# Raw input into the first two P1 products, its row factor put in at their eviction, and three steps of the last pair's products moved behind the scores

## The chip, the cores and the metric

The kernel runs on one core of one Trainium2 chip. The metric is the device time of one execution in microseconds (us); for the kernel before, it is the median of three runs. TensorE is PE in the rows of the profile, VectorE DVE, ScalarE ACT, GpSimd POOL, and SyncE SP.

## What is computed

Two encoder layers over 512 tokens of width 2048, in float32. Each layer normalises its rows, multiplies by one wide input weight, runs three groups of heads (latent attention, a gated short convolution, attention into 256 memory tokens), gates them and multiplies by an output weight. What the change touches is the first line of a layer and its first products:

```python
def rmsnorm(x, g):
    x32 = x.astype(jnp.float32)
    y = x32 * lax.rsqrt(jnp.mean(x32 * x32, axis=-1, keepdims=True) + EPS)
    return (y * g.astype(jnp.float32)).astype(x.dtype)

    for l in range(DEPTH):
        h = rmsnorm(x, pre_norm_g[l])
        z = h @ w_in[l]
        q_lat, kv_lat, k_pe, gb, gc, xin, q_mem, gate = split_cols(z)
        ...
        a_out = mla_attention(q, k, v)
        ...
        y = jnp.concatenate([a_out, c_out, m_out], axis=-1) * jax.nn.silu(gate)
        o = y @ w_o[l]
        x = x + rmsnorm(o, post_norm_g[l])
```

The row factor of the norm, one number per token, multiplies a whole row. So it can be put in ahead of a product with the weight or behind it.

## The kernel before

**Precision.** Every float32 operand is split into a high part (a rounded copy, made by ACT) and a low part (the rest, made by DVE). A product is three matmuls, high by high, high by low, low by high (`mm3`, lines 250 to 254, so every product shows up as L252, L253 and L254). For a weight block these are `wh` (L177) and `wl` (L178), for the left operand the two lines of `split_to` (L257 and L258).

**Blocks.** The input and the output products are done with seven products of blocks in place of eight (Strassen's scheme). The left operand is cut into halves of the tokens and halves of the contraction: A11, A12, A21, A22, with the sums S1 to S4 made from them by `combine`. P1 multiplies A11, P2 multiplies A12, P5 multiplies S1, and so on (`LEFT`). Each half of the tokens is two tiles of 128 tokens. A `group` covers two column blocks of the weight. For the first two groups of a layer (form `HEAD`) P1 and P2 of both groups come first, and P5 and the rest of both groups after that, because S1 to S4 need the second half of the tokens. A product has four steps of one weight block each (256 rows of the contraction), each step does both token tiles, and each token tile takes six matmuls, so a step is twelve matmuls. The first two steps of the very first P1 are one (`two`): tile 0 by two weight blocks, then tile 1. When a product ends, `ended` evicts its PSUM bank: P1 of these groups is copied by ACT (L464), P2 is added to it by DVE (L457).

**The order.** All steps are recorded by `add` and run by `Program.run` in that order. A step's weight block is loaded some units ahead and prepared (split) two units ahead. TensorE, SP and POOL take their instructions in the recorded order; for ACT and DVE this holds until `first.close`, and after it a scheduler picks their order. Small work such as `combine` and the splits is put into a queue (`pr.defer`) with a cost, and is taken from it as steps with `room` go by, or at once where a product asks for an operand (`pr.until` in `products`). SP carries the loads, POOL carries loads that add to a tile in place (`more`), and the short row factor computation.

**The start.** Per tile of 128 tokens: `first_load` brings x, `first_factor` sums its squares on ACT (L563) and makes the factor on POOL, `first_rows` multiplies on DVE (L613), `transpose_rows` turns it on TensorE (L582) and evicts it with the gain of the norm, by DVE (L584) or ACT (L588), and `left_half` splits it. TensorE turns an identity 60 times meanwhile (`warm`, L1208).

**The end of attention.** `pipeline` runs one iteration per head and query block: the score of iteration k, whatever stands between, the transposes of iteration k-3 (L1002), and for every other one the product with V of iteration k-5. For the last pair of heads, what stands between is P2 of both groups of the output projection, one step per iteration:

```python
        last_pair = {0: [(sums(0), []), g0[0][0]], 1: [g0[0][1]], 2: [g0[0][2]], 3: [g0[0][3]],
                     4: [g1[0][0]], 5: [g1[0][1]], 6: [g1[0][2]], 7: [g1[0][3]]}
```

The pair has eight iterations, 0 to 7. From 8 on no score is left.

## Time and profile before

| | us |
|---|---|
| median of three runs | 1514.81 (1514.28 to 1516.2) |
| the profiled execution | 1515.76 |
| its span, first to last instruction | 1514.0 |
| TensorE busy in it | 1488.7 (98%) |
| DVE busy | 1065.3 (70%) |
| ACT busy | 863.7 (57%) |
| POOL busy | 287.5 (19%) |

The span is counted from the first instruction of the program to the last; the time of an execution has some more around it. Rows of the timeline give the start and the length in us, the engine, the source line, the operation, what is written from what, the shapes and how often; a bracket gives the idle time ahead of it and what ended that. A matmul's length is its way through the array; consecutive ones overlap, so that the distance of their starts is their cost.

### The profile page before, as it was taken

What the parts mean: (1) busy time and instruction counts of PE and PEld (TensorE: products, weight loads), DVE (VectorE), ACT (ScalarE), POOL (GpSimd) and SP (SyncE); (2) the same over time, 40 slices, a digit from 0 to 9 for tenths busy, and PEclk for the clock granted to TensorE, in tenths of its full rate; (3) what the DMA queues carried; (4) which work ended last, traced back from release to release, by engine and by line L of the source; (5) the groups of instructions that cost most, each with busy time, mean ns of one, the idle gap of its engine ahead of it and who ended that gap; (6) DMA issues with size and microseconds to landing.
All of it is one profiled execution on the core that took longest, in us unless ns stands there. A gap on an engine that the chain in (4) does not pass through costs nothing.

```text
span 1514.0 us, 20209 instructions
## 1 busy us (share of the span) xinstructions
PE 1488.7 (98%) x7613; PEld 1277.7 (84%) x7613; DVE 1065.3 (70%) x1422; ACT 863.7 (57%) x1335; POOL 287.5 (19%) x289
## 2 busy tenths in 40 slices
PE   9999999999999999999999999999999999999997
PEld 7788888988898888878788888888988888888885
DVE  6965675565877668769788765675565586688687
ACT  7743534454667768644588533534454587686443
POOL 1233131332000000230220233131333000003111
PEclk9999999999999999999999999999999999999999
DMA  8999898989582111595987999898989521137945
GB/s 329 218 220 224 194 176 169 201 198 250 164 267 76 48 42 57 106 213 155 319 290 236 237 220 222 197 173 171 205 194 213 152 70 43 29 90 138 260 111 181
DMA packets 142581, 267.19 MB, mean 176 GB/s; under 512 B 17084, under 2 KB 39956, under 8 KB 139156
## 3 DMA queue, kind: packets, MB, share of 16 engines
q0 software_dynamic: 59072, 128.99, 44.5%
q1 hardware_dynamic: 83280, 136.88, 28.1%
q8 instruction: 59, 0.97, 0.3%
q14 instruction: 38, 0.31, 0.1%
q10 hardware_dynamic: 132, 0.05, 0.0%
HBM read 251.20 MB, written 14.68 MB: 176 GB/s over the span
## 4 chain that ended last, share of the span: by engine, by line
PE 83%; DVE 6%; issue 4%; ACT 3%; POOL 2%; DMA 1%; POOLq 0%; DVEq 0%; ACTq 0%
PE P L253 20%; PE P L254 20%; PE P L252 20%; PE ptp L1002 2%; PE tps L758 2%; DVE wl L178 1%; PE o L253 1%; PE sc L252 1%; PE sc L253 1%; PE sc L254 1%; PE o L254 1%; PE o L252 1%; POOL wr L137 1%; PE sc L982 1%; PE sc L983 1%
## 5 line engine op out<-in xcount | busy, mean ns | idle before, releaser
L178 DVE TENSOR_TENSOR wl<-wr,wh 128x1024 fp32r<-128x1024 f32 (+1 forms) x400 | 476.0, 1194 | 303.5 <-ACT wh L177 302.7
L177 ACT CAST wh<-wr 128x1024 fp32r<-128x1024 f32 (+1 forms) x400 | 411.9, 1032 | 475.5 <-PE P L254 397.0
L253 PE MATMUL P<-wl,S 128*128 128x512 f32 (+1 forms) x896 | 344.2, 384 | 2.9 <-DVE wl L178 2.8
L252 PE MATMUL P<-wh,S 128*128 128x512 f32 (+1 forms) x896 | 346.1, 386 | 0.0
L254 PE MATMUL P<-wh,S 128*128 128x512 f32 (+1 forms) x896 | 343.5, 383 | 0.0
L137 POOL DMA_DIRECT2D wr<-in_w_in_dram x160 | 193.5, 1209 | 484.4 <-DVE wl L178 380.3
L252 PE MATMUL P<-wh,A 128*128 128x512 f32 (+1 forms) x656 | 253.1, 386 | 0.6 <-ACT wh L177 0.6
L253 PE MATMUL P<-wl,A 128*128 128x512 f32 (+1 forms) x656 | 251.9, 384 | 1.5 <-DVE wl L178 1.5
L254 PE MATMUL P<-wh,A 128*128 128x512 f32 (+1 forms) x656 | 251.6, 384 | 0.5 <-DVE A L258 0.5
L253 PEld LDWEIGHTS P<-wl,S 128*128 128x128 f32 x896 | 168.3, 188 | 33.6 <-DVE wl L178 4.5
L254 PEld LDWEIGHTS P<-wh,S 128*128 128x128 f32 x896 | 168.2, 188 | 30.6
L252 PEld LDWEIGHTS P<-wh,S 128*128 128x128 f32 x896 | 168.1, 188 | 29.6 <-ACT wh L177 0.3
L137 POOL DMA_DIRECT2D wr<-in_w_o_dram x40 | 48.4, 1209 | 527.4 <-DVE rec L990 352.1
L253 PEld LDWEIGHTS P<-wl,A 128*128 128x128 f32 x656 | 123.2, 188 | 23.6 <-DVE wl L178 2.1
L254 PEld LDWEIGHTS P<-wh,A 128*128 128x128 f32 x656 | 123.1, 188 | 23.4 <-DVE A L258 1.2
L252 PEld LDWEIGHTS P<-wh,A 128*128 128x128 f32 x656 | 123.1, 188 | 23.1 <-ACT wh L177 1.5
L988 ACT ACTIVATE P<-sc,nm 128x512 f32<-128x512 f32 (+1 forms) x96 | 60.0, 625 | 36.4 <-DVE nm L985 35.8
L991 ACT ACTIVATE P<-P,rec 128x512 f32<-128x512 f32 (+1 forms) x96 | 62.1, 658 | 5.1 <-DVE rec L990 5.1
L985 DVE TENSOR_REDUCE nm<-sc 128x1 f32<-128x512 f32 (+1 forms) x96 | 57.1, 595 | 10.0 <-PE sc L983 6.2
L258 DVE TENSOR_TENSOR PT<-ptp,PT 128x512 fp32r<-128x512 f32 (+1 forms) x96 | 56.4, 593 | 8.5 <-ACT PT L257 8.1
L182 ACT ACTIVATE wh<-wr,cols 128x512 fp32r<-128x512 f32 x64 | 44.2, 721 | 19.9 <-PE mk L253 7.4
L183 DVE SCALAR_TENSOR_TENSOR wl<-wr,cols,wh 128x512 fp32r<-128x512 f32 x64 | 46.3, 746 | 12.4 <-ACT wh L182 12.2
(272 smaller groups left out, 2225.2 us busy)
## 6 DMA issues: line engine op xcount, KB each, us to landing
wr<-in_w_in_dram POOLq DMA_DIRECT2D x128, 512.0 KB, 6.9
wr<-in_w_in_dram SPq DMA_DIRECT2D x112, 512.0 KB, 5.4
wr<-in_w_o_dram SPq DMA_DIRECT2D x48, 512.0 KB, 4.2
wr<-in_w_o_dram POOLq DMA_DIRECT2D x40, 512.0 KB, 7.3
wr<-in_w_in_dram POOLq DMA_DIRECT2D x32, 416.0 KB, 5.4
wr<-in_w_in_dram SPq DMA_DIRECT2D x24, 416.0 KB, 4.2
wr<-in_w_mk_dram SPq DMA_DIRECT2D x16, 512.0 KB, 4.9
wr<-in_w_mv_dram SPq DMA_DIRECT2D x16, 512.0 KB, 4.9
```

The source lines that it names most:

```text
L137: engine.dma_start(dst, src, **kw)
L177: nc.scalar.copy(hi[:, :n], src)
L178: nc.vector.tensor_tensor(lo[:, :n], src, hi[:, :n].bitcast(F32), op=ALU.subtract)
L182: nc.scalar.activation(hi[:, h], src[:, h], AF.Copy, scale=g)
L183: nc.vector.scalar_tensor_tensor(lo[:, h], src[:, h], g, hi[:, h].bitcast(F32), op0=ALU.mult, op1=ALU.subtract)
L252: nc.tensor.matmul(ps, ah, bh, start=first, stop=False, **kw)
L253: nc.tensor.matmul(ps, ah, bl, start=False, stop=False, **kw)
L254: nc.tensor.matmul(ps, al, bh, start=False, stop=last, **kw)
L258: nc.vector.tensor_tensor(lo, src, hi.bitcast(F32), op=ALU.subtract)
L985: nc.vector.tensor_reduce(nmax, ps, axis=AX.X, op=ALU.max, negate=True)
L988: nc.scalar.activation(pt, ps, AF.Exp, bias=nmax, accum_out=tot)
L991: nc.scalar.activation(pt, pt, AF.Copy, scale=rec)
```

## The change

- The first two tiles are loaded by halves of the columns, with weight blocks between them. Their first halves are turned as they come, without a factor, in quarters that are split one by one (`turn_raw`, `split_raw`). So A11 is raw for P1 of the first two groups of layer 0, and the eviction of these P1 multiplies by the row factor on ACT (`factor`).
- The square sums, factors and scaled second halves of these tiles come later. 28 warm-up transposes take the place of 60, and the second step of the first P2 is joined too (`k < 2`).
- `combine` needs the scaled first halves. Their turned form is multiplied in place by the factors, which are spread over a PSUM bank by two transposes (`spread_factors`, `scale_half`); A11 is split a second time, scaled, after the second group's P1.
- The constants are split into two loads; those of the memory norm and the convolution are issued by SP behind the fourth tile, and turned after the first P2.
- In both layers the last three steps of P2 of the output's second group go from iterations 5, 6, 7 to 8, 9, 10.

```diff
-            if by_two and k == 0:
+            if by_two and k < 2:
                 steps[:2] = [(two(names[0], 0), [unit(names[0], c) for c in range(2)], 0.0, 1)]
...
-                if apart:
+                if apart and factor:
+                    nc.scalar.activation(s[1, 0], ps, AF.Copy, scale=factor(tt))
+                elif apart:
                     nc.scalar.copy(s[1, 0], ps)
...
+    def spread_factors():
+        ps = G["rows01"] = bank("rps")
+        for t in range(2):
+            wide = scrap("factors", P)
+            nc.vector.tensor_copy(wide, G[f"r{t}"].broadcast_to([P, P]))
+            nc.tensor.transpose(ps[:, t * P:(t + 1) * P], wide, G["ident"])
+
+    def scale_half(t, h):
+        r = G["rows01"][:, t * P:(t + 1) * P].rearrange("p (o c) -> p o c", o=1).broadcast_to([P, 8, P])
+        nc.vector.tensor_tensor(h, h, r, op=ALU.mult)
...
     add(setup)
+    add(lambda: first_load(0, (0,)))
+    add(pr.begin_loads(1))
+    add(lambda: first_load(1, (0,)))
+    add(pr.begin_loads(2))
     for t in range(2):
-        add(lambda t=t: first_load(t))
-        add(lambda t=t: first_factor(t))
-        if t == 0:
-            add(lambda: first_rows(0))
-    add(pr.begin_loads(3))
+        add(lambda t=t: first_load(t, (1,)))
+        add(pr.begin_loads(3 + t))
+    add(pr.begin_loads(6))
     add(lambda: first_load(2))
-    add(pr.begin_loads(5))
+    add(pr.begin_loads(8))
     add(lambda: first_load(3))
-    add(lambda: warm(60))
-    add(turn_constants)
+    add(constants_load)
+    add(lambda: warm(20))
+    add(pre_gains)
...
-            add(turn_half(0, 0))
-            add(lambda: first_rows(1, (0,)))
+            def turn_raw(t, q, on=None):
+                return lambda: transpose_rows(0, t, G[f"x{t}"], (q,), on)
+            def split_raw(t, q):
+                return lambda: G["left"].split("A11", t, G[f"hT{t}"][:, 4 * q:4 * q + 4, :], slice(4 * q, 4 * q + 4))
+            add(turn_raw(0, 0))
+            add(turn_raw(0, 1))
+            add(split_raw(0, 0))
             add(pr.begin_prep(1))
-            add(lambda: left_half(0, (0,)))
+            add(split_raw(0, 1))
+            add(lambda: warm(8))
+            add(turn_raw(1, 0))
             add(pr.begin_prep(2))
-            add(turn_half(1, 0, nc.scalar))
-            add(lambda: first_rows(1, (1,)))
-            add(lambda: left_half(1, (0,)))
+            add(turn_raw(1, 1, nc.scalar))
+            add(split_raw(1, 0))
+            add(split_raw(1, 1))
             add(pr.begin_prep(3))
-            add(lambda: first_factor(2))
-            add(turn_half(0, 1))
+            add(lambda: first_factor(0))
...
             put(a[:1])
             add(first.close)
-            add(turn_half(1, 1))
+            add(lambda: first_rows(0, (1,)))
+            add(lambda: first_factor(1))
+            add(lambda: first_rows(1, (1,)))
+            put(a[1:2])
+            add(turn_half(0))
             add(lambda: left_half(0, (1,)))
+            put(a[2:])
+            add(turn_half(1))
             add(lambda: left_half(1, (1,)))
+            add(lambda: first_factor(2))
             add(lambda: first_rows(2))
             add(lambda: first_factor(3))
             add(lambda: first_rows(3))
-            put(a[1:], b[:1])
+            put(b[:1])
+            add(spread_factors)
+            first_half = {}
+            def scale(t):
+                h = first_half[t] = G[f"hT{t}"][:, :8, :]
+                pr.defer(1.2, lambda: scale_half(t, h))
+            add(lambda: scale(0))
+            add(lambda: scale(1))
             add(turn[2])
             add(lambda: right_half(0))
-            put(b[1:3])
+            put(b[1:2])
             add(turn[3])
             add(lambda: right_half(1))
-            put(b[3:])
+            put(b[2:])
+            add(other_constants)
...
-        put(a1, b1)
+        put(a1, b1[:1])
+        if l == 0:
+            for t in range(2):
+                add(lambda t=t: pr.defer(1.2, lambda: G["left"].split("A11", t, first_half[t])))
+            add(lambda: pr.defer(0.0, lambda: G.update(whole=True)))
+        put(b1[1:])
         put(*gs[0][2:], *gs[1][2:])
+        if l == 0:
+            add(lambda: pr.until(lambda: 'whole' in G))
...
-                     4: [g1[0][0]], 5: [g1[0][1]], 6: [g1[0][2]], 7: [g1[0][3]]}
+                     4: [g1[0][0]], 8: [g1[0][1]], 9: [g1[0][2]], 10: [g1[0][3]]}
```

More of the change, by code (lines that the diff above doesn't have):

```diff
@@ L278, in setup, with constants_load, turn_constants, pre_gains @@
         G.update(ident=identr.bitcast(F32), identr=identr, mhalf=mhalf, junk=const.tile([P, 512], mybir.dt.bfloat16, name="junk"))
-        rows = scrap("rows", P)[:KT * 2 * depth + 12 * depth]
+        rows = G["rows"] = scrap("rows", P)
+        nc.scalar.dma_start(rows[:KT * depth], pre_norm_g.rearrange("l (k p) -> (l k) p", p=P))
+    def constants_load():
+        rows = G["more"] = scrap("more", P)
         n = KT * depth
-        nc.scalar.dma_start(rows[:n], pre_norm_g.rearrange("l (k p) -> (l k) p", p=P))
-        nc.scalar.dma_start(rows[n:2 * n], mem_norm_g.rearrange("l (k p) -> (l k) p", p=P))
-        nc.scalar.dma_start(rows[2 * n:], conv_w.rearrange("l k (c p) -> (l k c) p", p=P))
-        G["rows"] = rows
-    def turn_constants():
-        rows = G["rows"]
-        n = KT * depth
-        m = 2 * n + 12 * depth
-        ps = bank("cps")
-        nc.tensor.transpose(ps[:, :m], rows, G["ident"][:m, :m])
-        cols = const.tile([P, m], F32, name="cols")
-        nc.vector.tensor_copy(cols, ps[:, :m])
+        nc.sync.dma_start(rows[:n], mem_norm_g.rearrange("l (k p) -> (l k) p", p=P))
+        nc.sync.dma_start(rows[n:n + 12 * depth], conv_w.rearrange("l k (c p) -> (l k c) p", p=P))
+    def turn_constants(name, n):
+        ps = bank("cps")
+        nc.tensor.transpose(ps[:, :n], G[name][:n], G["ident"][:n, :n])
+        cols = const.tile([P, n], F32, name=f"cols{name}")
+        nc.vector.tensor_copy(cols, ps[:, :n])
+        return cols
+    def pre_gains():
+        cols = turn_constants("rows", KT * depth)
         for l in range(depth):
             G[f"g1_{l}"] = cols[:, l * KT:(l + 1) * KT]
-            G[f"gm_{l}"] = cols[:, n + l * KT:n + (l + 1) * KT]
-            G[f"cw{l}"] = cols[:, 2 * n + 12 * l:2 * n + 12 * (l + 1)].rearrange("p (k c) -> p k c", k=3)
+    def other_constants():
+        n = KT * depth
+        cols = turn_constants("more", n + 12 * depth)
+        for l in range(depth):
+            G[f"gm_{l}"] = cols[:, l * KT:(l + 1) * KT]
+            G[f"cw{l}"] = cols[:, n + 12 * l:n + 12 * (l + 1)].rearrange("p (k c) -> p k c", k=3)
     def positions_load():
@@ L377, in __init__, with split @@
             self.ops = {}
-        def split(self, name, p, src):
-            t = self.ops[name, p] = slab(f"{name}{p}", F32R)
+        def split(self, name, p, src, ks=slice(None)):
+            if (name, p) not in self.ops:
+                self.ops[name, p] = slab(f"{name}{p}", F32R)
             c = src.shape[-1]
-            split_to(t[:, :1024].rearrange("p (k c) -> p k c", c=c), t[:, 1024:].rearrange("p (k c) -> p k c", c=c), src)
+            hi, lo = (self.ops[name, p][:, h * 1024:(h + 1) * 1024].rearrange("p (k c) -> p k c", c=c) for h in range(2))
+            split_to(hi[:, ks], lo[:, ks], src)
         def there(self, name, kt, tt):
@@ L414, in encoder, with group @@
     LATE = [["P2"], ["P1"], ["P5", "P6", "P3"], ["P7"], ["P4"]]
-    def group(left, key, w, block, slot, passes, final, hold=None, by_two=False):
+    def group(left, key, w, block, slot, passes, final, by_two=False, factor=None, hold=None):
         bk = {}
@@ L600, in right_half, with first_load @@
         combine(left, tt, a[:, :8, :], a[:, 8:, :], b[:, :8, :], b[:, 8:, :])
-    def first_load(t):
-        xt = G[f"x{t}"] = slab("x")
-        nc.sync.dma_start(xt, x[0, t * P:(t + 1) * P, :])
+    def first_load(t, halves=(0, 1)):
+        if f"x{t}" not in G:
+            G[f"x{t}"] = slab("x")
+        if len(halves) == 2:
+            nc.sync.dma_start(G[f"x{t}"], x[0, t * P:(t + 1) * P, :])
+        for h in halves if len(halves) == 1 else ():
+            c = slice(h * 1024, (h + 1) * 1024)
+            nc.sync.dma_start(G[f"x{t}"][:, c], x[0, t * P:(t + 1) * P, c])
     def first_factor(t):
@@ L656, in projection @@
         L = G["left"]
+        rf = (lambda tt: G[f"r{tt}"]) if l == 0 else None
         gs = [
-            group(L, (l, 0), 512, block((O_GC, O_XI), 512), slot_of("gc", "xi"), HEAD, fin_u, by_two=l == 0),
-            group(L, (l, 1), 512, block((O_GB, O_G + 1024), 512), slot_of("gb", "gg"), HEAD, fin_g),
+            group(L, (l, 0), 512, block((O_GC, O_XI), 512), slot_of("gc", "xi"), HEAD, fin_u, l == 0, rf),
+            group(L, (l, 1), 512, block((O_GB, O_G + 1024), 512), slot_of("gb", "gg"), HEAD, fin_g, factor=rf),
             group(L, (l, 2), 512, block((O_G + 1536, O_QM), 512), slot_of("gm", "qm"), STEADY, skip),
@@ L1166, in out_proj @@
         g0 = group(G["left"], ("o", l, 0), 512, block(0), slot(0), SECOND, fin(0))
-        g1 = group(G["left"], ("o", l, 1), 512, block(1), slot(1), LATE, fin(1), hold if last else None)
+        g1 = group(G["left"], ("o", l, 1), 512, block(1), slot(1), LATE, fin(1), hold=hold if last else None)
         return g0, g1, gains, fetch
@@ L1250, in encoder @@
             add(use)
-            def turn_half(t, h, on=None):
-                return lambda: transpose_rows(0, t, G[f"hs{t}"], (2 * h, 2 * h + 1), on)
-            add(turn_half(0, 0))
-            add(lambda: first_rows(1, (0,)))
+            def turn_raw(t, q, on=None):
[5 more added lines that the diff above has]
+            add(split_raw(0, 0))
             add(pr.begin_prep(1))
-            add(lambda: left_half(0, (0,)))
+            add(split_raw(0, 1))
+            add(lambda: warm(8))
+            add(turn_raw(1, 0))
             add(pr.begin_prep(2))
-            add(turn_half(1, 0, nc.scalar))
-            add(lambda: first_rows(1, (1,)))
-            add(lambda: left_half(1, (0,)))
+            add(turn_raw(1, 1, nc.scalar))
+            add(split_raw(1, 0))
+            add(split_raw(1, 1))
             add(pr.begin_prep(3))
-            add(lambda: first_factor(2))
-            add(turn_half(0, 1))
+            add(lambda: first_factor(0))
         else:
@@ L1282, in encoder, with turn_half @@
         if l == 0:
+            def turn_half(t):
+                return lambda: transpose_rows(0, t, G[f"hs{t}"], (2, 3))
             put(a[:1])
             add(first.close)
-            add(turn_half(1, 1))
+            add(lambda: first_rows(0, (1,)))
[3 more added lines that the diff above has]
+            add(turn_half(0))
             add(lambda: left_half(0, (1,)))
+            put(a[2:])
+            add(turn_half(1))
             add(lambda: left_half(1, (1,)))
+            add(lambda: first_factor(2))
             add(lambda: first_rows(2))
```

## The prediction

> **What bounds the kernel now.** I read the page first, then busy time by stretches, then TensorE's own waits, then the timeline of three places: the first 20 us, the stretch around 37 to 67 us, and the end of the last pair of heads.

> ```profile
> PE 1488.7 (98%) x7613; PEld 1277.7 (84%) x7613; DVE 1065.3 (70%) x1422; ACT 863.7 (57%) x1335; POOL 287.5 (19%) x289
> ...
> PE 83%; DVE 6%; issue 4%; ACT 3%; POOL 2%; DMA 1%; POOLq 0%; DVEq 0%; ACTq 0%
> ```
> ```profile
> 0.00:15.28 15.28, 12.06 (x85) 11.82 (x86) 5.62 (x9) 8.64 (x10) 2.24 (x11) 1.00 0.88 339
> 15.28:37.48 22.20, 21.70 (x109) 17.73 (x108) 17.82 (x21) 20.28 (x40) 1.67 (x4) 1.00 0.91 320
> 37.48:61.45 23.97, 22.98 (x109) 18.71 (x108) 23.22 (x22) 18.69 (x32) 5.06 (x4) 1.00 0.88 216
> 61.45:76.00 14.55, 14.55 (x65) 12.03 (x65) 14.52 (x14) 9.04 (x10) 6.06 (x5) 1.00 1.09 227
> ...
> 1503.80:1514.00 10.20, 0.00 (x0) 0.00 (x0) 4.87 (x7) 0.72 (x2) 0.74 (x2) 0.75 0.53 206
> ```
> ```profile
> PE P L253 <- DVE wl L178: 4.4, 5, 1.0
> PE o L253 <- DVE PT L258: 2.0, 4, 0.7
> ```

> TensorE has work for 98% of the span and the chain of waits runs over it. So a time can change only where TensorE stands still, or by added TensorE work. It stands still in three kinds of places: before the first product (the first 15.28 us hold only warm-up and turning), after the last product (10.20 us, which this change does not touch), and in short waits of at most 1.0 us. But the third number to see is DVE's: 23.22 of 23.97 us, then 14.52 of 14.55 us. From 37 to 76 us DVE is as full as TensorE, and the change adds DVE work exactly there. (Columns of the middle fence: stretch, its length, then busy us and instructions of TensorE, its weight loads, DVE, ACT and POOL, then granted clock, DMA share and GB/s.)

> **The change part by part.** First the start.

> ```profile
> 1.61:5.88 4.27, 4.26 (x20) 4.27 (x21) 0.00 (x0) 1.28 (x1) 0.00 (x0) 1.00 0.91 329
> ...
> 7.02:10.70 3.68, 3.68 (x35) 3.68 (x34) 1.42 (x2) 3.12 (x5) 0.87 (x3) 1.00 1.02 389
> ```
> ```profile
> 1.62 9.38 PE L1208 MATMUL warm<-identr 128*128 128x128 f32 x60 [1.62 <-DVE identr L275]
> ...
> 5.92 1.91 ACT L563 ACTIVATE hs<-x 128x2048 f32<-128x2048 f32 x1 [2.32 <-DMA x<-in_x_dram]
> ...
> 8.48 1.92 ACT L563 ACTIVATE hs<-x 128x2048 f32<-128x2048 f32 x1 [0.56 <-DMA x<-in_x_dram]
> ...
> 10.39 1.03 ACT L177 CAST wh<-wr 128x1024 fp32r<-128x1024 f32 x1
> ...
> 11.11 0.25 DVE L293 COPY cols<-cps 128x88 f32<-128x88 f32 x1 [0.83 <-PE cps L291]
> 11.55 1.29 DVE L584 TENSOR_TENSOR hT<-hps,cols 128x512 f32<-128x512 f32 x2 [0.19 <-PE hps L582]
> ...
> 12.88 1.05 ACT L257 CAST A<-hT 128x1024 fp32r<-128x1024 f32 x1 [1.45 <-DVE hT L584]
> 13.42 1.22 DVE L178 TENSOR_TENSOR wl<-wr,wh 128x1024 fp32r<-128x1024 f32 x1
> ...
> 15.28 0.47 PE L252 MATMUL P<-wh,A 128*128 128x512 f32 x1
> ...
> 15.60 0.40 PE L253 MATMUL P<-wl,A 128*128 128x512 f32 x1
> ...
> 18.23 0.39 PE L252 MATMUL P<-wh,A 128*128 128x512 f32 x1
> ...
> 18.45 0.39 PE L253 MATMUL P<-wl,A 128*128 128x512 f32 x1
> ...
> 19.34 0.50 PE L254 MATMUL P<-wh,A 128*128 128x512 f32 x1 [0.50 <-DVE A L258]
> ```

> Before, the first product waits for a chain: tile 0 landed (5.92), square sum, factor, scaling, turning, split. After, turning needs only the raw first half. A tile of 1 MB takes 2.56 us of transfers (8.48 - 5.92), so its first half is there about 1.3 us before 5.92, at 4.6, and the first weight block behind it at 5.9. Neither limits: TensorE turns when its 20 warm-up transposes end, at 5.9 by the window of 4.26 us. Then four transposes at that rate (0.21 each, to 6.8), an eviction of 512 columns (half of 1.29, to 7.5), the high part of a half (half of 1.05, to 8.1), the weight's high part (1.03, to 9.1), with some 0.04 us per hand-over (11.55 + 1.29 = 12.84 to 12.88): first product at 9.3. **Start: -6.0 us.**

> Not all of that is kept, because the queues of ACT and DVE behind it are no shorter. The second matmul needs the low weight part, 1.22 us after 9.3, while only one matmul (they follow each other by 0.23, as 18.23 to 18.45) lies between: wait of 0.9. DVE then has a half low part (0.6), an eviction (0.6) and the second block's low part (1.22): ready at 12.9, wanted at 12.0: wait of 0.9. Before lost 0.7 here (18.45 to 19.34, less 0.23). **P1: +1.1 us.**

> ```profile
> 18.89 1.91 ACT L563 ACTIVATE hs<-x 128x2048 f32<-128x2048 f32 x1
> ...
> 21.75 1.03 PE L582 MATMUL hps<-identr,hs 128*128 128x128 f32 x8
> ...
> 37.48 1.22 DVE L178 TENSOR_TENSOR wl<-wr,wh 128x1024 fp32r<-128x1024 f32 x1 [2.96 <-ACT wh L177]
> ...
> 60.20 1.22 DVE L397 TENSOR_TENSOR hT<-hT 128x1024 f32<-128x1024 f32 x1
> ...
> 62.59 1.22 DVE L178 TENSOR_TENSOR wl<-wr,wh 128x1024 fp32r<-128x1024 f32 x1
> ...
> 63.73 1.22 DVE L258 TENSOR_TENSOR S<-hT,S 128x1024 fp32r<-128x1024 f32 x1
> ...
> 66.00 1.27 DVE L457 TENSOR_TENSOR gb<-gb,P 128x512 f32<-128x512 f32 x2
> ...
> 67.17 0.39 PE L252 MATMUL P<-wh,S 128*128 128x512 f32 x1
> ```

> Second halves. Eight transposes of tile 0's second half, which stood ahead of the first product, now stand inside P1, as tile 1's already did: 1.0 (the row at 21.75). The two wide factor transposes and the second constants transpose add 0.3. The square sums of both tiles (1.91 each) now come on ACT after the first splits, and the second halves are scaled, turned and split only then. ACT, from 9.1 with a step of about 1.0 each: half of A, the second weight block, four small evictions, two halves of A, the third block (13.8), two sums (17.6), two blocks (19.6). DVE follows with their low parts (21.7), two evictions (22.9), one more weight part (24.0) and only then A12's low part, 25.2. TensorE comes to P2 at 24.1 (9.3 + 48 x 0.23 + 1.8 of waits + 16 transposes, 2.0) and wants that low part two matmuls later, 24.5: wait of 0.7 to 0.8, and the same again for tile 1, whose evictions stand behind it. Before, P2 did not wait. **+1.3 and +1.5 us**, so TensorE comes into the second group some 2.1 us early (-6.0 + 1.1 + 1.3 + 1.5). The short wait at that group's first step, the longest of the 4.4 us above, stays: the weight split there stands behind the same turning.

> P5 is where this ends. Its second tile needs S1 of tile 1: a subtraction on DVE, a cast on ACT, a low part on DVE. Before, DVE ran from 37.48 to the subtraction at 60.20 over 20 instructions without a real gap, and the low part was ready at 64.95 (63.73 + 1.22). TensorE asked for tile 1 at 67.17, for the low part two matmuls later, 67.6: 2.7 us to spare. In the changed program's order DVE hardly starts this stretch earlier. At 37.48 it had waited for ACT, which had been busy 20.28 of the 22.20 us before; the two square sums that ACT did ahead of 10.4 (3.8 us) now lie in that stretch, and of the sixteen turned quarters that ACT evicts there none is dropped, so the 6.0 us are eaten. Between there and the same subtraction it now has three 1024-wide instructions more (the scaled A11's low part of tile 0, and two weight parts that formerly stood behind) and the two 512-wide evictions of P2 that stood at 66.00, and a small copy. 1024-wide ones follow each other by 1.14 (62.59 to 63.73), 512-wide ones by 0.6 (two in 1.27), the copy takes 0.2 (the row at 11.11): 3 x 1.14 + 2 x 0.6 + 0.2 = 4.8 us later. So the low part is ready at 69.7, wanted at 67.6 - 2.1 = 65.5; less what the slightly earlier start takes off, a wait of about 3.6 to 4.2. I take 3.6, as the 0.75 us that DVE was idle there (23.97 less 23.22) will be filled. **P5: +3.6 us.** After the first 76 us the account is -2.1 + 3.6 = +1.5. With TensorE gapless behind it, nothing gives that back.

> At no cost: the eviction of P1 with a factor (some 0.1 us more on ACT for 512 columns, four times, and no product waits for it); the factor itself (sums done by 17.6, wanted when P1 ends, past 22); constants on SP behind the fourth tile (two short issues; the weight loads behind them wait for buffers that DVE frees anyway; the gains are used far later).

> Last pair, in each layer:

> ```profile
> 619.52 0.69 ACT L988 ACTIVATE P<-sc,nm 128x512 f32<-128x512 f32 x1 [1.56 <-DVE nm L985]
> ...
> 620.66 0.73 ACT L991 ACTIVATE P<-P,rec 128x512 f32<-128x512 f32 x1
> 621.32 1.04 PE L1002 MATMUL ptp<-identr,P 128*128 128x128 f32 x8
> ...
> 624.25 1.08 ACT L257 CAST PT<-ptp 128x512 fp32r<-128x512 f32 x2 [0.23 <-PE ptp L1002]
> ...
> 625.56 1.28 DVE L258 TENSOR_TENSOR PT<-ptp,PT 128x512 fp32r<-128x512 f32 x2
> ...
> 625.80 0.28 PE L254 MATMUL o<-PT,V 128*128 128x256 f32 x1
> 625.92 0.28 PE L252 MATMUL o<-PT,V 128*128 128x256 f32 x1
> ...
> 626.89 0.39 PE L253 MATMUL o<-PT,V 128*128 128x256 f32 x1 [0.70 <-DVE PT L258]
> ```

> Before, the last head's transposes and products run with nothing between, and the last product waits 0.85 plus a slow restart of 0.1 for the low part of PT (625.92 to 626.89, less the 0.12 by which such products follow each other). After, a P2 step of twelve matmuls (12 x 0.23 = 2.7 us) stands ahead of each of the last three transposes, so ACT and DVE have cleared the earlier tiles: that wait goes, -0.95. The step's removal takes 2.7 us of cover from three score rounds. There the TensorE work of a round falls to five matmuls (1.14), four transposes (0.5) and on average six products (0.7), 2.3 us; ACT has 0.69 + 0.73 + 0.54 (half of 1.08) and DVE the maximum and a low part, under 2.2 us, plus a deferred cast now and then. They keep up only just, and I put one wait of 0.4 to 0.6 per layer there (nearest row: the 0.70 above); below zero it cannot go, as a wait is no gain. **Last pair: -0.4 us per layer, -0.8.** On POOL's queue the first accumulating loads wait for weight parts that are now made two steps (5.4 us) later; they are due when P5 begins, behind P1's four steps, 10.9 us on.

> Sum: +1.5 - 0.8 = +0.7, and +1.3 with the upper end of P5's wait. I take **+1.2 us**, near the upper end, as any hand-over or landing later than placed here lengthens the chain of ACT and DVE up to P5. The profiled execution took 1515.76 (span 1514.0 and 1.76 around it), so 1517.0 for its like; the median of the runs is 0.95 lower, 1514.81, so **1516.0**.

> The clock. Twenty transposes took 4.26 us, later thirty-five took 3.68: the array doubled its rate at about 7.0 us, having run transposes alone, and the products of 15.28 and 15.60 on are at full rate. The change cuts the warm-up from 60 to 28, but with the real ones TensorE is busy from 1.6 to 9.1 us, past 7.0.
> [...]

> **The rivals.**
> *DVE keeps up* (8%). If S1 of tile 1 and both A12 come in time, 3.6 + 1.5 us fall away: 1510.9. For: at 61.45:76.00 TensorE never waited though DVE was full. Against: the order on DVE puts 4.8 us more ahead of that subtraction.
> *The uncovered scores become the bound* (8%), the slower case. If ACT and DVE fall behind by a deferred cast (1.05) in each of the three bare score rounds, TensorE waits 0.9 per round instead of once: 2.7 per layer in place of 0.5, so +4.4: 1520.4. It decides once ACT lags by more than the three rounds that lie between a score and its transpose. For: ACT's round is within 0.2 us of TensorE's. Against: before, ACT stood idle 1.56 us ahead of 619.52.
> *The start is not early* (6%). If the half tiles interleaved with weights land 2.7 us later than I place them, the whole ACT and DVE chain up to P5 shifts with them: 1518.7. Against: DMA moved 389 GB/s there, and the first half tile and weights (4.6, 5.9) are wanted at 5.9 and 8.1.
> *Cold products* (4%). If the gate is still closed at 9.3, matmuls take twice their time for as long as the rise took here, 1.6 to 7.0, so half of 5.4 us is lost, less the 1.8 us of waits that it would fill: +0.9 to 2.7, 1517.8.

> **How the numbers follow.** The forecast has 74%. One measurement of this kernel tells about 0.2% (3.0 us) from no change. Faster by that needs both of DVE's waits gone: 8%. Slower: the bare scores 8%, most of the late start 5%, 2% from a forecast whose P5 wait is twice mine: 15%. Within: 77%. The range reaches from P5's wait gone (1516.0 - 3.6 = 1512.4) up to the late start with some more (1519.2).

> **What would show it.** Right: first product at 9 to 10 us; two waits of 0.7 to 1 us on low weight parts in P1; waits of P2 on A12; near 65 to 70 us a wait of 3 to 4 us in all on S; DVE without a gap from 37 us; no wait on PT in the last product. Wrong: no wait on S (faster), waits on sc or ptp summing to over 2 us per layer (slower), or matmuls over 0.4 us apart after 9 us.

## The result, and the profile after

| | before | after |
|---|---|---|
| median of 7 runs | 1514.81 us (1513.83 to 1516.2) | 1520.6 us (1518.3 to 1526.73) |
| profiled execution | 1515.76 us | 1518.3 us, the fastest of its seven |
| its span | 1514.0 us | 1516.5 us |

The ratio is 1.0042 with a 95% interval of 1.0026 to 1.0057: slower by 5.8 us between the medians, where 1.2 was forecast. The mean granted TensorE clock is printed with each run: before it was 0.997 or 0.998, after it was 0.997 in the run of 1518.3 us, 0.996 in two of 1519.9 us, and 0.995 in the other four.

On the profile's page of the changed kernel nothing of that is seen; the shares of busy time are unchanged:

```profile
PE 1488.5 (98%) x7584; PEld 1274.5 (84%) x7584; DVE 1070.5 (71%) x1430; ACT 864.7 (57%) x1335; POOL 288.0 (19%) x289
...
PE 82%; DVE 6%; ACT 4%; issue 3%; DMA 2%; POOL 2%; POOLq 0%; DVEq 0%; ACTq 0%
```

TensorE's own waits, grouped (engine, line, tile, what it waited for; total us, times, longest):

```profile
PE P L253 <- DVE wl L178: 4.9, 7, 1.0
PE P L252 <- ACT S L257: 1.9, 1, 1.9
...
PE P L254 <- DVE S L258: 1.6, 1, 1.6
...
PE P L254 <- DVE A L258: 1.0, 2, 0.5
PE o L253 <- DVE PT L258: 1.0, 4, 0.3
```

Two rows on S are new, each a single wait: the two halves of P5's wait for S1 of tile 1. The wait on PT has halved. Next the timeline of TensorE in four places: the first products, P2, P5, and the stretch right behind it.

```profile
9.32 0.48 PE L252 MATMUL P<-wh,A 128*128 128x512 f32 x1
10.22 0.50 PE L253 MATMUL P<-wl,A 128*128 128x512 f32 x1 [0.42 <-DVE wl L178]
...
12.55 0.50 PE L253 MATMUL P<-wl,A 128*128 128x512 f32 x1 [0.70 <-DVE wl L178]
...
25.38 0.50 PE L254 MATMUL P<-wh,A 128*128 128x512 f32 x1 [0.53 <-DVE A L258]
...
28.92 0.50 PE L254 MATMUL P<-wh,A 128*128 128x512 f32 x1 [0.49 <-DVE A L258]
...
64.84 0.39 PE L254 MATMUL P<-wh,S 128*128 128x512 f32 x1
67.08 0.50 PE L252 MATMUL P<-wh,S 128*128 128x512 f32 x1 [1.85 <-ACT S L257]
67.42 0.39 PE L253 MATMUL P<-wl,S 128*128 128x512 f32 x1
69.41 0.50 PE L254 MATMUL P<-wh,S 128*128 128x512 f32 x1 [1.60 <-DVE S L258]
69.75 0.39 PE L252 MATMUL P<-wh,S 128*128 128x512 f32 x1
69.98 0.44 PE L253 MATMUL P<-wl,S 128*128 128x512 f32 x1
70.22 0.63 PE L254 MATMUL P<-wh,S 128*128 128x512 f32 x1
70.65 0.63 PE L252 MATMUL P<-wh,S 128*128 128x512 f32 x1
...
73.21 0.58 PE L252 MATMUL P<-wh,S 128*128 128x512 f32 x1
73.63 0.39 PE L253 MATMUL P<-wl,S 128*128 128x512 f32 x1
```

Down to 69.75 this is the forecast: first product at 9.3, two waits in P1, two in P2, P5's wait in two pieces (2.0 us between 64.84 and 67.08 beyond the usual 0.23, and 1.8 us). What was not in the forecast comes then: from 70.2 to 73.2 us matmuls follow each other by 0.43 us instead of 0.23, and nothing is waited for. Eight of them cost 1.6 us.

Busy time by stretches of 3.41 us, laid so that the two changes of the granted clock (70.19 and 73.61 us) fall on their edges (columns: stretch, its length, busy us and instructions of TensorE, its weight loads, DVE, ACT, POOL, then granted clock, DMA share, GB/s):

```profile
63.37:66.78 3.41, 1.86 (x9) 1.20 (x7) 3.41 (x5) 1.85 (x2) 1.93 (x2) 1.00 1.09 294
66.78:70.19 3.41, 1.51 (x5) 0.97 (x6) 3.41 (x4) 0.25 (x1) 1.20 (x1) 1.00 1.13 209
70.19:73.61 3.42, 3.42 (x9) 2.63 (x8) 3.04 (x4) 1.99 (x2) 0.00 (x0) 0.50 1.13 206
73.61:77.02 3.41, 3.41 (x16) 2.80 (x15) 2.81 (x3) 1.05 (x1) 1.22 (x1) 1.00 0.61 93
```

The granted clock is 0.50 for one stretch of 3.41 us, right behind a stretch in which TensorE was busy for only 1.51 us, and it is full again after a stretch in which TensorE never paused. Nine matmuls ran in it where sixteen run in the next.

### The profile page after: what moved, and what is told of

Read it like the earlier page. It is cut to its first block, busy times and chain, and to the rows that moved or that the text cites. A ratio compares the mean times of both kernels' runs of the same rounds, so it can differ in the third digit from the quotient of the medians.

```text
span 1516.5 us, 20173 instructions
## 1 busy us (share of the span) xinstructions
PE 1488.5 (98%) x7584; PEld 1274.5 (84%) x7584; DVE 1070.5 (71%) x1430; ACT 864.7 (57%) x1335; POOL 288.0 (19%) x289
## 4 chain that ended last, share of the span: by engine, by line
PE 82%; DVE 6%; ACT 4%; issue 3%; DMA 2%; POOL 2%; POOLq 0%; DVEq 0%; ACTq 0%
PE P L253 20%; PE P L254 20%; PE P L252 19%; PE ptp L1035 2%; DVE wl L178 2%; PE tps L791 1%; PE o L253 1%; ACT wh L177 1%; PE o L254 1%; PE o L252 1%; PE sc L252 1%; POOL wr L137 1%; PE sc L253 1%; PE sc L254 1%; PE qps L253 1%
## 5 line engine op out<-in xcount | busy, mean ns | idle before, releaser
L178 DVE TENSOR_TENSOR wl<-wr,wh 128x1024 fp32r<-128x1024 f32 (+1 forms) x400 | 476.3, 1195 | 307.9 <-ACT wh L177 305.6
L177 ACT CAST wh<-wr 128x1024 fp32r<-128x1024 f32 (+1 forms) x400 | 411.7, 1033 | 484.1 <-PE P L254 404.4
L252 PE MATMUL P<-wh,S 128*128 128x512 f32 (+1 forms) x896 | 346.8, 387 | 1.9 <-ACT S L257 1.9
L253 PE MATMUL P<-wl,S 128*128 128x512 f32 (+1 forms) x896 | 344.6, 385 | 2.3 <-DVE wl L178 2.3
L254 PE MATMUL P<-wh,S 128*128 128x512 f32 (+1 forms) x896 | 344.3, 384 | 1.6 <-DVE S L258 1.6
L253 PE MATMUL P<-wl,A 128*128 128x512 f32 (+1 forms) x656 | 252.2, 385 | 2.7 <-DVE wl L178 2.6
L252 PE MATMUL P<-wh,A 128*128 128x512 f32 (+1 forms) x656 | 253.7, 387 | 0.4 <-ACT wh L177 0.4
L254 PE MATMUL P<-wh,A 128*128 128x512 f32 (+1 forms) x656 | 251.7, 384 | 1.0 <-DVE A L258 1.0
L253 PEld LDWEIGHTS P<-wl,S 128*128 128x128 f32 x896 | 168.7, 188 | 33.0 <-DVE wl L178 3.6
L254 PEld LDWEIGHTS P<-wh,S 128*128 128x128 f32 x896 | 168.5, 188 | 32.8 <-DVE S L258 2.0
L252 PEld LDWEIGHTS P<-wh,S 128*128 128x128 f32 x896 | 168.5, 188 | 31.8 <-ACT S L257 2.3
L253 PEld LDWEIGHTS P<-wl,A 128*128 128x128 f32 x656 | 123.2, 188 | 25.5 <-DVE wl L178 4.4
L254 PEld LDWEIGHTS P<-wh,A 128*128 128x128 f32 x656 | 123.1, 188 | 24.1 <-DVE A L258 1.9
L252 PEld LDWEIGHTS P<-wh,A 128*128 128x128 f32 x656 | 123.1, 188 | 22.3 <-ACT wh L177 0.8
L258 DVE TENSOR_TENSOR PT<-ptp,PT 128x512 fp32r<-128x512 f32 (+1 forms) x96 | 56.9, 594 | 7.7 <-ACT PT L257 7.3
L182 ACT ACTIVATE wh<-wr,colsmore 128x512 fp32r<-128x512 f32 x64 | 44.2, 721 | 19.9 <-PE mk L253 7.6
L183 DVE SCALAR_TENSOR_TENSOR wl<-wr,colsmore,wh 128x512 fp32r<-128x512 f32 x64 | 46.4, 749 | 12.4 <-ACT wh L182 11.0
```

Of the source, the lines that this page charges most:

```text
L177: nc.scalar.copy(hi[:, :n], src)
L178: nc.vector.tensor_tensor(lo[:, :n], src, hi[:, :n].bitcast(F32), op=ALU.subtract)
L182: nc.scalar.activation(hi[:, h], src[:, h], AF.Copy, scale=g)
L183: nc.vector.scalar_tensor_tensor(lo[:, h], src[:, h], g, hi[:, h].bitcast(F32), op0=ALU.mult, op1=ALU.subtract)
L252: nc.tensor.matmul(ps, ah, bh, start=first, stop=False, **kw)
L253: nc.tensor.matmul(ps, ah, bl, start=False, stop=False, **kw)
```

## Experiments

**The changed kernel twice more, for its profile alone.** The first theory was that the slower runs lose more such stretches. No edit.

> The changed kernel itself, for a second profile: its profiled execution was the fastest of seven (1518.3 us at a mean granted clock of 0.997), the others lay at 0.996 or 0.995 and 1519.9 to 1526.7. Theory (the clock): every execution loses whole stretches of 3.4 us at half rate, 1.7 us each; the profiled one had one, at 70.1 us, behind P5's wait. A run at 0.996 should show two such stretches and 1520.0, a run at 0.995 three and 1521.6, each of them behind a place where TensorE waited in the first 76 us. Rival (something else varies, such as DMA): the time differs from 1518.3 with the same single half-rate stretch, and the extra time shows as waits.

> The changed kernel, for a third profile. Theory (the clock): one or two half-rate stretches of 3.4 us that begin at the end of a stretch in which TensorE stood still for over 2.0 us in P5's waits on S, one if the stretch behind it is fully busy, two if it still holds part of the wait; at 1.7 us each on 1516.6 us: 1518.3 or 1520.0 us, up to 1 us more by DMA waits. Rival: stretches at half rate elsewhere.

They took 1521.09 and 1520.97 us. Of the first:

```profile
65.57:68.98 3.41, 0.86 (x3) 0.30 (x2) 3.41 (x4) 1.04 (x1) 1.17 (x2) 1.00 1.10 270
68.98:72.39 3.41, 2.51 (x6) 2.05 (x7) 3.11 (x3) 0.35 (x1) 0.23 (x1) 0.50 1.14 208
72.39:75.81 3.42, 3.42 (x9) 2.68 (x9) 2.70 (x3) 1.64 (x2) 1.05 (x1) 0.50 0.81 147
75.81:79.22 3.41, 3.41 (x16) 2.81 (x16) 2.02 (x2) 1.05 (x1) 0.17 (x1) 1.00 0.76 108
```

Two stretches at half rate, both behind P5's wait, and none elsewhere ahead of the last product; the third profile has the same picture, from 68.38 to 75.21. The waits are the same size as in the first profile; where the clock falls within them differs. Here it falls at 68.98 us and not at 70.19. The stretch of 65.57 to 68.98 caught most of the wait (0.86 of 3.41 us busy); the next one (2.51 of 3.41 busy) still held its end, and was followed by another at half rate. The matmuls of the two half-rate stretches cost 2.7 to 2.9 us instead of 1.6 to 1.8. So the theory holds, but not its detail that a granted clock of 0.995 means three stretches: the third profile has 0.995 and two. The mean also counts the end of the execution, where the clock is at half from some 5 us behind the last product on (from 1508.9 us in the first profile of before, 1510.6 in that of after), at no cost; so its third digit does not count stretches. The rest of the distance to 1518.3 lies in waits of 0.3 to 1.7 us behind 330 us, most of them on weights, which differ from execution to execution in both kernels.

**The wait filled.** 32 spare transposes stand on TensorE where it waits for S1 of tile 1:

```
 for tt in range(2):
+    if key == (0, 0) and q == "P5" and c == 0 and tt == 1:
+        for k in range(32):
+            nc.tensor.transpose(bk[q][1][:, :P], G["ident"], G["ident"])
     products(q, c, tt, ops[0])
```

> The changed kernel with 32 spare transposes (0.107 us each, 3.4 us) on TensorE in the place where P5 waits for S of tile 1; they fill the wait and bring no data. Theory (the clock closes because TensorE stands still there): no half-rate stretch near 70 us; if all lost stretches come from that wait, 1516.6 us and a granted clock of 0.998 in every run. Second form (some of them come from the waits of the first 30 us): one stretch fewer, 1518.9 us, 0.996 to 0.997. Rival (the scatter has nothing to do with that wait): 1520.6 us and the clock as it was.

```profile
65.16:68.57 3.41, 3.41 (x32) 3.28 (x31) 3.41 (x5) 1.24 (x2) 1.01 (x2) 1.00 1.10 275
68.57:71.99 3.42, 3.22 (x18) 2.41 (x16) 3.42 (x4) 0.93 (x1) 0.70 (x1) 1.00 1.14 208
```

No half-rate stretch; the granted clock is 0.997 to 0.998 in all eleven runs. The median is 1518.23 us, ratio to before 1.0018 (1.0009 to 1.0027), against 1.0042 for the changed kernel: spare work that brings no data makes the kernel 2.4 us faster by the medians, 3.6 by the ratios (which hold the one run of 1526.73 us), and 2.9 by the medians of the spans (1518.8 and 1515.9), as some executions of this run had up to 3.4 us around the span where 1.8 is usual. S1 is ready no sooner, as the low part of tile 1 lets P5 go on at 69.79 us (69.41 to 69.88 in the three profiles of after), so this is the clock alone:

```profile
69.79 0.50 PE L254 MATMUL P<-wh,S 128*128 128x512 f32 x1 [0.20 <-DVE S L258]
```

The figure of 1516.6 was missed by 1.6 us: it had been taken from the fastest execution of the changed kernel.

**Half of the wait filled**, with 20 in place of 32:

> As the run with 32 spare transposes, with 20: they fill the first of P5's two waits (2.0 us) and leave the second (1.6 to 1.8 us). Theory (the clock falls when TensorE stands still for 2.0 us or more of a stretch of 3.4 us): the clock stays at 0.997 to 0.998, and the time is that of the run with 32, 1518.2 us. Rival (one wait of 1.6 us is enough): half-rate stretches as in the changed kernel, 1520.6 us.

```profile
64.12:67.54 3.42, 3.42 (x27) 3.08 (x25) 3.42 (x5) 1.86 (x2) 1.27 (x2) 1.00 1.11 285
67.54:70.95 3.41, 1.89 (x9) 1.31 (x8) 3.41 (x4) 0.30 (x1) 1.08 (x1) 1.00 1.13 208
70.95:74.36 3.41, 3.41 (x17) 2.83 (x16) 3.27 (x4) 2.71 (x3) 0.97 (x1) 1.00 1.09 199
```

One wait of 1.7 us is left, TensorE is busy for 1.89 of 3.41 us in the stretch that holds it, and the clock stays, at 0.997 to 0.998 in all eleven executions. 1517.22 us, ratio 1.0019 (1.0010 to 1.0027): by the ratio as with 32. The median is 1.0 us below the expected one, and that of before, timed beside it, was 0.7 lower too.

**The wait alone, with the old start.** In the kernel before, DVE is given three more 1024-wide operations ahead of tile 1's subtraction:

```
+        if late and p == 1:
+            for k in range(3):
+                put_off(nc.vector.tensor_tensor, a22, a22, a22, op=ALU.max)
         put_off(nc.vector.tensor_tensor, a22, a22, a21, op=ALU.subtract)
```

> The kernel before, with its old start and 60 warm-up transposes, and three more 1024-wide operations on DVE (each takes the larger of a tile and itself, so the data stay) ahead of the subtraction for S1 of tile 1. P5 then waits for tile 1's S1 by 3.6 to 4.8 us. Theory (that wait alone closes the clock): one or two half-rate stretches near 73 us, granted clock 0.995 to 0.997, 1514.9 + 4.2 + 2.4 = 1521.5 us. Rival (the clock falls only with the new start's shorter warm-up or its waits): clock 0.998 and 1519.1 us.

```profile
66.58:69.99 3.41, 0.18 (x1) 0.18 (x2) 3.38 (x4) 1.04 (x1) 1.40 (x2) 1.00 1.10 202
69.99:73.41 3.42, 3.19 (x7) 2.03 (x8) 3.35 (x3) 0.12 (x1) 0.00 (x0) 0.50 1.12 200
73.41:76.82 3.41, 3.41 (x16) 2.82 (x15) 2.64 (x4) 3.41 (x4) 0.81 (x1) 1.00 0.20 38
```

1520.68 us, ratio 1.0044 (1.0031 to 1.0057), granted clock 0.996 to 0.997; 1521.5 had been expected. P5 waits 3.5 us in one piece here and another 0.4 for the low part. The new start, its 28 warm-up transposes and the waits of its first 30 us are not needed for a half-rate stretch; a late S1 is enough. But this wait leaves TensorE busy for only 0.18 us of a stretch. That the two shorter waits of the changed kernel close the clock there is shown by the two runs that fill them.

**One part at a time.** The last pair alone, and the start alone (steps of the second group behind iterations 8, 9, 10 in the first, 5, 6, 7 in the second):

```
-                     4: [g1[0][0]], 5: [g1[0][1]], 6: [g1[0][2]], 7: [g1[0][3]]}
+                     4: [g1[0][0]], 8: [g1[0][1]], 9: [g1[0][2]], 10: [g1[0][3]]}
```

> Only the last pair of heads is changed (second group's steps behind iterations 8, 9, 10), the start is that of before. Theory (start and clock carry the loss): the wait on PT in the last product goes, in both layers, 0.4 us each, and the DMA wait of 1.0 us near 680 us goes as it did in the changed kernel: 1513.0 to 1514.0 us at a granted clock of 0.998. Rival (the bare score rounds cost the time): waits on sc or ptp, 1517 to 1520 us.

> Only the start is changed; the last pair is that of before. Theory (the start's waits and the clock carry the loss): P5's wait on S of 3.8 us, half-rate stretches behind it, granted clock 0.995 to 0.997, and 0.8 to 1.8 us more than the changed kernel: 1521.4 to 1522.4 us, and above all the same scatter. Rival (the last pair carries the loss): 1515.5 to 1517 us at 0.998.

The last pair alone: 1513.77 us, ratio 0.9994 (0.9985 to 1.0003), clock 0.998 in ten of eleven runs. The start alone: 1521.01 us (1521.4 to 1522.4 expected), ratio 1.0034 (1.0021 to 1.0046), clock 0.995 to 0.997. The loss is the start's. TensorE's waits in the last pair of the first:

```profile
PE o L253 <- DVE PT L258: 1.0, 4, 0.3
PE sc L252 <- DVE rm L885: 0.8, 2, 0.4
PE ptp L1002 <- ACT P L988: 0.6, 2, 0.3
```

The wait on PT went from 2.0 to 1.0 us over both layers, and sc and ptp wait no longer than before (0.8 and 0.7 us): the bare score rounds did not become the bound.

**The wait taken away.** The deferred work of layer 0 in another order: subtraction and S1 of tile 1 come right behind those of tile 0, ahead of tile 0's S2, S4 and S3; the split of tile 1's A22 stays ahead of them, other than the expectation below says. The cut is abridged, its comment stands for code.

```
 put_off(nc.vector.tensor_tensor, a22, a22, a21, op=ALU.subtract)
 split("S1", a22)
+# what follows (S2, S4, S3) goes to a list, called once both tiles have come this far
...
-add(lambda: right_half(1))
+add(lambda: right_half(1, later))
+add(lambda: [f() for f in later])
```

> The changed kernel with its deferred work in another order: in layer 0 the subtraction and split for S1 of tile 1 are queued right behind those of tile 0, ahead of tile 0's S2, S4 and S3 and of tile 1's A22. Nothing is left out. Theory (P5's wait is DVE's queue, and the clock falls because of that wait): the waits of 2.0 and 1.8 us on S go, no half-rate stretch near 70 us, the granted clock is 0.998; some 0.5 us of wait comes on P6 in their place; 1518.2 (the run with filled waits) less 3.3 = 1514.9 us. Rival (DVE is behind by as much anyway): P6 and P3 wait for S2 or S4 by about 3 us instead, the clock falls there, and the time stays at 1518 to 1521 us.

P5's wait is gone and no stretch of the profile is at half rate ahead of the last product. But P6 waits by more than the 0.5 us expected:

```profile
76.07 0.39 PE L253 MATMUL P<-wl,S 128*128 128x512 f32 x1
78.23 0.50 PE L254 MATMUL P<-wh,S 128*128 128x512 f32 x1 [1.77 <-DVE S L258]
```

1515.55 us, ratio 1.0011 (1.0002 to 1.0020): 1.7 us faster than the run with 20 transposes, which was timed beside it, close to the 3.8 us that went less the 1.9 that came; still 1.3 behind before. Half of the rival was right: in this order the low part of tile 1's S2 comes 1.9 us late at P6 instead. DVE's queue is not all of that, as DVE itself stood idle for 1.35 us ahead of 68.94, waiting for a cast of ACT. Two further orders, the first abridged in the same way (ACT takes one more eviction, the second split of A11 comes later):

```
-                return lambda: transpose_rows(0, t, G[f"hs{t}"], (2, 3))
+                # tile 0: quarter 2 evicted by ACT, quarter 3 by DVE
...
-        put(a1, b1[:1])
+        put(a1, b1)
+        put(*gs[0][2:4])
         (second split of A11 deferred here)
```

> As the order with S1 of tile 1 first, and two more moves: ACT instead of DVE evicts the first quarter of tile 0's second half, and the second split of A11 is queued behind P6 and P3 instead of behind P2. Nothing is left out. Theory: the wait on A12 of tile 0 near 25 us (0.7 us) falls to 0.2; 0.4 to 0.6 us less than the run with S1 first, so about 1514.4 us, 0.5 below the kernel before. Rival: ACT has no room there, the wait moves to tile 1's A12 and the time is that of the run with S1 first.

1515.52 us, ratio 1.0009 (1.0000 to 1.0018): the time that the rival gave, 1.1 us above the theory's. The wait on A12 of tile 0 went, the one on tile 1's stayed as it was (0.7 us), and P6 still waits 1.9 us. Then S3 of both tiles behind S2 and S4 of both:

> The previous order (S1 of both tiles first, A11 late, first quarter of tile 0's second half on ACT), and S3 of both tiles queued behind S2 and S4 of both. Nothing is left out. Theory (DVE's queue only): the wait of 1.9 us on S2 of tile 1 at P6 (75.3 us) goes and nothing takes its place: 1515.5 less 1.9 = 1513.6 us, 0.6 to 1.2 below the kernel before. Rival (the early start pays for itself only in waits elsewhere): 1515.5 us as the run with S1 first.

1513.75 us, ratio 0.9992 (0.9982 to 1.0001). P6 no longer waits, and the time fell by 1.8 us (1.9 expected), though the kernel before, timed beside each, was 0.8 us slower here (1515.04 and 1514.21). It includes the new last pair, which alone gives 0.9994. Neither can be told from the kernel before, so the early start is worth nothing that these runs can show, even when its waits behind P2 are gone.

The profile of this run shows one place where the gain goes. At the matmul that before reaches at 80.9 us (mean of its three profiles) TensorE is 1.8 us early, and it still is at 354 us. Near 679 us the last pair's gain should have come on top, but ACT has waited 5.24 us for the DMA of an output weight, and TensorE waits twice for that weight's parts:

```profile
677.88 2.95 ACT L177 CAST wh<-wr 128x1024 fp32r<-128x1024 f32 x3 [5.24 <-DMA wr<-in_w_o_dram]
```
```profile
678.98 0.50 PE L252 MATMUL P<-wh,S 128*128 128x512 f32 x1 [0.65 <-ACT wh L177]
680.24 0.50 PE L253 MATMUL P<-wl,S 128*128 128x512 f32 x1 [0.76 <-DVE wl L178]
```

At 748 us the lead is 0.6 us, and another wait of that kind near 1424 us takes most of the rest. Whether a lead always ends there is open; it was not tested.

In one execution of each of these three orders the granted clock is as low as with half-rate stretches: 0.996 at 1517.11 and 1518.52 us, 0.995 at 1519.09. These three have no trace, so what lowered it is not known.

**The kernel before twice more**, as its first profile was above its median:

> The kernel before itself, for a second profile. Theory: its first profile (span 1514.0) was not a typical one; its first product can come at 14.4 us as in the run with late S1 (not 15.3), and the wait of 1.0 us near 680 us is there in some executions only, so the span here is 1512.4 to 1513.1. Rival: the start is at 15.3 us and the wait at 680 us is there each time, and what is left of the loss lies behind the start of the changed kernel.

> The kernel before once more, for a third profile; theories and numbers as for the second.

```profile
14.61 0.48 PE L252 MATMUL P<-wh,A 128*128 128x512 f32 x1
```
```profile
14.92 0.48 PE L252 MATMUL P<-wh,A 128*128 128x512 f32 x1
```

1515.13 us (span 1513.4) and 1514.61 us (1512.8). The first product starts at 14.61 and 14.92 us, with 15.28 in the first profile; and the wait of 1.0 us near 680 us is there in the second profile (0.8) but not in the third. The theory holds in part: the start moves by 0.7 us between these executions (the two experiments with the old start have 14.36 and 15.53), and one of the two spans lies where it was expected (1512.4 to 1513.1).

## Why the prediction was wrong

**The steps that stood.** From the first product to the third matmul of P5's tile 1, three profiles of before took 52.3 us (to 67.63 in the first), and three of after took 60.1 us (9.32 to 69.41). The added 7.8 us were forecast as 1.1 + 1.3 + 1.5 + 3.6 = 7.5. The waits are the ones named: P1's at 9.5 and 11.7, A12's at 24.7 and 28.3, and S's by 3.8. The queue of DVE was read right; its rows in after, from that subtraction on:

```profile
64.73 1.22 DVE L408 TENSOR_TENSOR hT<-hT 128x1024 f32<-128x1024 f32 x1
65.87 1.22 DVE L178 TENSOR_TENSOR wl<-wr,wh 128x1024 fp32r<-128x1024 f32 x1
67.01 1.22 DVE L408 TENSOR_TENSOR hT<-hT,hT 128x1024 f32<-128x1024 f32 x1
68.14 1.22 DVE L258 TENSOR_TENSOR S<-hT,S 128x1024 fp32r<-128x1024 f32 x1
```

As forecast, DVE does the 20 instructions of before from 37.44 us to the subtraction, and one low part of a left block (A), two low parts of weights, two evictions and one copy more. The subtraction starts at 64.73, 4.5 us later than the 60.20 of before (4.8 forecast), and the low part of S1 is ready at 69.36 (69.7 forecast). The eviction of P1 with the factor took 0.69 us on ACT, without it 0.59 (0.1 more forecast). The last pair brought 0.5 us per layer (0.4 forecast).

**A term mis-sized.** "Start: -6.0 us" took the first product of before from one profile, at 15.28, the latest of three. With all three the mean is 14.94 (so it is with the two experiments that have the old start), and 9.59 for after (9.32, 9.81, 9.63): -5.35 us.

**The step that failed** is the end of the account of the first 76 us: the wait of P5 was charged at its own length and then "with TensorE gapless behind it, nothing gives that back". Nothing gives it back, but the wait also takes something more: the clock behind it, 1.8 us in one profile of after and 2.7 to 2.9 in the two others, 2.4 us by the run with the wait filled (2.9 by its spans). The prediction had half-rate matmuls in view, in the rival "cold products" (the granted clock still at half, its "gate" closed, when the first product comes), at 4%. It placed them only at 9.3 us, asked only whether the clock had come up by then, and never asked of the new wait of 3.6 us whether the clock would stay up through it. Its own sign for that ("matmuls over 0.4 us apart after 9 us") is what the trace shows, 61 us later than it was looked for.

The account over three profiles each: -5.35 + 7.8 + 2.45 (mean of the clock's 1.8, 2.9, 2.7) = +4.9 us, and the matmul that before reaches at 80.9 us comes 4.85 us later in the profiles of after. The last pair takes 1.0 off, +3.9 us. The last product starts at 1507.5 us on average, before at 1502.8: +4.6 us. The 0.7 us between belongs to waits, most of them on weights, behind 330 us that change between executions of either kernel (0.7 us near 686 us in one profile of after and not in the others, 1.7 near 1428 in another, 1.0 and 0.8 near 680 in two of before and none in the third). Another 1.2 us from there to the 5.8 us between the medians stays open: three profiles of each are too few to say that the changed kernel has more of these waits.

**The other rivals.** DVE did not keep up; the bare scores did not become the bound; the start was not late.

What the loss went with in these traces, TensorE's busy time in the 3.41 us ahead of a fall of the clock, the prediction did not weigh; the last section has the figures. Transposes were enough to hold the clock: the 32 spare ones fill a stretch (3.41 of 3.41 us busy), and the next one is still at 1.00.

## What to carry to other kernels

When a change makes TensorE wait, look at how long it stands still in all within some 3.4 us (one half-rate stretch here), not only at the longest wait: two waits of 2.0 and 1.8 us close together here cost their length and then 1.6 to 2.9 us of half-rate matmuls, more in some executions than in others, while one of 1.7 us alone cost only its length. If the wait can't be removed by another order of the work, fill it with spare transposes, which took 2.4 us off the median here. And take the time of a start that hangs on DMA landings from more than one profile: this one moved by 0.7 us between three.

## What the runs showed of the hardware

```profile
10.43:13.84 3.41, 1.80 (x18) 1.57 (x17) 2.53 (x5) 1.96 (x4) 0.75 (x2) 1.00 1.06 419
```

Of the stretches looked at, none lies between 1.51 and 1.80 us. The fall in the first profile of after came with two gaps of 2.0 and 1.8 us and matmuls between them; parts of both fell into one stretch that was still busy for 1.51 us.

Half-rate stretches busy for 3.19 (the late S1 with the old start), 3.41 (third profile of after) and 3.42 us (the other two) were followed by the full clock; those busy for 2.51, 2.35 (68.79 to 72.20 us of the run with the start alone) and 2.10 us (68.38 to 71.80 us of the third profile of after) were followed by another at half rate. The clock fell at 70.19, 68.98 and 68.38 us in the three profiles of after, and the same wait cost one stretch, 1.8 us, in the first, and two, 2.7 to 2.9 us, in the others. The one run of 1526.73 us, at the same granted clock as its neighbours, is not explained.
